# Mixed operands of the first query quad in four steps, key rotation as side work, and VectorE for GpSimd in the operand and rotation work

## The chip, the cores and the metric

The kernel runs on one core of one Trainium2 chip. The metric is the time of one execution on the device in microseconds; the kernel before takes 1295.9 us (median of three runs, 1295.33 to 1296.37).

## The reference

The input `x` is 512 tokens by 1024, float32. One layer is a half-weighted SwiGLU feed-forward block with a layer norm, a token mixer with a layer norm, and a second such feed-forward block.

```python
def swiglu(x, w1, w3, w2):
    return (jax.nn.silu(x @ w1) * (x @ w3)) @ w2
...
    proj = h @ w_in + b_in
    q_a, k_a, v_a, f_h, q_h, i_h, og_h, gate_a, gate_h = jnp.split(proj, splits, axis=-1)
    q_a = partial_rope(q_a.reshape(B, S, N_Q_HEADS, HEAD_DIM), cos, sin)
    k_a = partial_rope(k_a.reshape(B, S, N_KV_HEADS, HEAD_DIM), cos, sin)
    y_attn = sliding_window_attention(q_a, k_a, v_a, sinks)
...
    merged = jax.nn.sigmoid(gate_a) * (y_attn @ w_pa) + jax.nn.sigmoid(gate_h) * (y_hgrn @ w_ph)
    return merged @ w_out
...
    x = layer_norm(DEEPNORM_ALPHA * x + 0.5 * swiglu(x, ffn1_w1[l], ffn1_w3[l], ffn1_w2[l]), ...)
    mix = token_mixer(x, w_in[l], b_in[l], ...)
    x = layer_norm(DEEPNORM_ALPHA * x + mix, ...)
    x = layer_norm(DEEPNORM_ALPHA * x + 0.5 * swiglu(x, ffn2_w1[l], ffn2_w3[l], ffn2_w2[l]), ...)
```

Attention has 16 query heads and 4 key heads of 64, in blocks of 128 tokens with a window of 128 and a learned sink. `y_hgrn` is a gated linear recurrence over eight heads. `partial_rope` rotates the first 16 of each head's 64 entries: with `t` the projection, it is `t * cos + swap(t) * sin`, where `swap` exchanges two groups of eight.

## The kernel before

**Products.** Every float32 operand of a large product is held as a rounded part `hi` and a remainder `lo`; the product is made of three passes, hi by hi, hi by lo and lo by hi. `split` (line 72) makes them: ACT casts to `hi` (line 74), DVE subtracts it from the source to give `lo` (line 75). For weights the names are `whi` and `wlo`, `raw` is the weight as it was loaded (a ring of five), and `wsum` a sum of two of them or a temporary.

**Quads.** The projections of 512 columns by 1024 rows are made with seven products in place of eight (class `Quads`). The activations are cut in four, `b11`, `b12`, `b21`, `b22`, and four mixtures of them are needed too:

```python
t1 = b11 - b12;  t2 = -t1 - b22;  t3 = b22 - b12;  t4 = -t2 - b21
```

`X.mixed` (line 131) forms them on DVE and splits each (`fin`, line 126) into the operands `x1.op["t1"]` to `["t4"]`. The lower part of `t3` and `t4` is formed on GpSimd (POOL), those of `t1` and `t2` on DVE. Its temporaries are rooms of `wsum`, of which there are three, used in turn by `t1`, `t2`, `t4`, `t3` and then by the weight sums. `mixed` is used three times: in the two feed-forward blocks (`ffn`, by way of `Quads.eight`), once each after a block of four products, and in the mixer just before the first query quad.

A quad takes its four raw weights, forms the sums `p1 = w21 + w22` and `p3 = w11 + w21` (`plus`, DVE, line 291), then `p2 = w22 + p3` and `p4 = w12 + p2`, and runs the products in this order, each of 24 matmuls on TensorE (PE, line 278), each with its own activation operand: `f1` (weight w11, operand b11), `f5` (p1, t1), `f6` (p2, t2), `f2` (w12, b21), `f7` (p3, t3), and then in the next quad's `flush` `m4` (w22, t4) and `m3` (p4, b22). After f1 its result is copied by ACT to a room `m` and after f6 to `vs` (`keep`, line 296), since f6 and f7 accumulate into the bank of f1: f6 can't begin before the copy `m` is done, and f7 not before `vs`. `Pipe` prepares one product ahead of the one that runs.

**The mixer's start.** The value projection and `k_half(0)`, `k_half(1)` (the keys, four column blocks in two banks `accs`) run on PE with matmuls of lines 106 to 108. Then stand, in the program, for both key tiles: the bias on ACT (line 646), the rotation (`rope`, lines 645 to 651: a shuffle on DVE, the product with the sines on POOL, the product with the cosines and the sum on DVE), four casts into `k_hi` (ACT, line 685) and two subtractions into `k_lo` (DVE, line 686); then `x1.mixed(quads.sum_room)` and `q_quad(0)`, the first query quad. Rotation of a query tile is the same `rope`; there are ten in all, two for the keys and eight for the queries.

**Order.** A scheduler puts the instructions of each engine in one list, and each engine takes its list in order. `Side` holds generators with small steps of work (rotation of the queries, scores, softmax, outputs) and takes `rate` of them after each product. Attention and the gate quads `gate_quad` (weights `w_ga`, `w_gh`) follow the first query quad so, and the second query quad `q_quad(1)` comes within them. `room(i)` and `big(i)` are buffers named `r` and `g` in the profile.

Of the kernel before, what the change touches and what calls it, by code (L numbers as in the profile page):

```python
# [15 lines left out]
ALU = mybir.AluOpType  # L16
# [26 lines left out]
def body(ctx, tc, a):  # L43
# [73 lines left out]
    class X:  # L117
# [13 lines left out]
        def mixed(self, room):  # L131
            pool = nc.gpsimd
# [3 lines left out]
            def tmp():  # L136
                return room().rearrange("p (k c) -> p k c", k=4)

            t1, t2 = tmp(), tmp()
            nc.vector.tensor_tensor(out=t1, in0=b11, in1=b12, op=ALU.subtract)  # L140
            nc.vector.scalar_tensor_tensor(out=t2, in0=t1, scalar=-1.0, in1=b22, op0=ALU.mult, op1=ALU.subtract)
            self.fin("t1", full, t1)
            t4 = tmp()
            nc.vector.scalar_tensor_tensor(out=t4, in0=t2, scalar=-1.0, in1=b21, op0=ALU.mult, op1=ALU.subtract)
            self.fin("t2", full, t2)
            t3 = tmp()
            nc.vector.tensor_tensor(out=t3, in0=b22, in1=b12, op=ALU.subtract)
            self.fin("t3", full, t3, pool)
            self.fin("t4", full, t4, pool)

# [101 lines left out]
    class Outs:  # L252
# [3 lines left out]
        def room(self, i):  # L256
            return self.rooms[i]
# [4 lines left out]
    class Quads:  # L262
# [60 lines left out]

        def quad(self, src, outs):


            w11, w21, w22, w12 = (raw(src[i]) for i in (0, 2, 3, 1))
            p1 = self.plus(w21, w22)
            p3 = self.plus(w11, w21)
            v, c, m1, vs, u3, p2, p4 = ([] for _ in range(7))  # L330

# [9 lines left out]
            def g2():  # L341
                p2.append(self.plus(w22, p3))
                return wsplit(p2[0])
# [271 lines left out]

    def quad_to(src, d1, d2, done=None):
# [5 lines left out]
        quads.quad(src, Outs((*thalves(d1), d2[:, :, 256:]), finish))  # L622

# [49 lines left out]
    k_hi = [big(i, dtype=F32R) for i in (4, 10)]
    k_lo = [big(i, dtype=F32R) for i in (2, 11)]
    for t in k_lo:
        nc.gpsimd.memset(t[top, 1].bitcast(F32), 0.0)
        nc.gpsimd.memset(t[bot, 0].bitcast(F32), 0.0)
    for j in range(2):  # L680
        t = room(6 + j)
        rope(accs[j], bias("k", j), 1.0, t)
        for h, own in enumerate((top, bot)):
            for half in (top, bot):
                nc.scalar.copy(out=k_hi[j][half, h], in_=t[own])
            nc.vector.tensor_tensor(out=k_lo[j][own, h], in0=t[own], in1=k_hi[j][own, h], op=ALU.subtract)
# [506 lines left out]
```

## Time and profile before

| | us |
|---|---|
| median of three runs | 1295.9 |
| profiled execution | 1297.03 |
| its span, first to last instruction | 1294.9 |
| PE busy | 1253.3 |
| DVE busy | 936.2 |
| ACT busy | 626.4 |
| POOL busy | 75.9 |

The span is the time from the first to the last instruction of the profiled execution, and 2.1 us of the execution lie outside it. The granted clock of TensorE was 0.995 on the mean. In a timeline row an idle time in brackets is what the engine waited before the row, and the name behind the arrow is the instruction whose end it waited for. A row may stand for several instructions of one kind; a matmul's row of eight 128x256 takes 1.12 us at full clock, that is 0.96 us from its first to the next row's start, 0.12 us for each matmul. Twelve matmuls are 1.44 us and a product is 2.88 us.

### The profile page before, as it was taken

The numbers are of one execution on the slowest core, as the hardware profiler recorded it, in microseconds if no ns is written. First come the engines' busy times: TensorE is split into PE (matmuls) and PEld (weight loads), VectorE is DVE, ScalarE is ACT, GpSimd is POOL, SyncE is SP. The second block draws the span as 40 slices with busy tenths as digits, with TensorE's granted clock in tenths as the row PEclk, the third lists the DMA queues.
The fourth block names the chain that finished last, engine by engine and source line by source line (L and its number), as shares of the span: only waits on it lengthen the run. The fifth ranks groups of instructions, "written<-read, shape, count | busy, mean of one in ns | idle before, by whom it ended". The sixth has DMA issues, their size and how long they took to land.

```text
span 1294.9 us, 21771 instructions
## 1 busy us (share of the span) xinstructions
PE 1253.3 (97%) x9040; PEld 1170.0 (90%) x9040; DVE 936.2 (72%) x1288; ACT 626.4 (48%) x891; POOL 75.9 (6%) x53
## 2 busy tenths in 40 slices
PE   7999999999998999999999999899999999999997
PEld 7999999988898989898998987788899999998886
DVE  7987878623499998997778776464798787784325
ACT  5645555411156667667653746342355445463110
POOL 2000000000031100100011010000120000000001
PEclk9999999999999999999999999999999999999998
DMA  6424233532233443223223243574233423354211
GB/s 239 134 96 131 83 114 131 179 96 88 94 104 105 144 134 99 91 98 101 71 77 102 83 130 122 168 255 131 98 115 115 128 85 115 102 162 143 84 47 65
DMA packets 53315, 150.75 MB, mean 116 GB/s; under 512 B 5856, under 2 KB 15072, under 8 KB 53216
## 3 DMA queue, kind: packets, MB, share of 16 engines
q1 hardware_dynamic: 49184, 135.72, 32.3%
q10 hardware_dynamic: 4032, 13.63, 3.0%
q8 instruction: 71, 1.16, 0.4%
q14 instruction: 28, 0.23, 0.1%
HBM read 134.65 MB, written 14.68 MB: 115 GB/s over the span
## 4 chain that ended last, share of the span: by engine, by line
PE 56%; DVE 7%; issue 2%; POOL 1%; ACT 1%; DMA 1%; DVEq 0%; SPq 0%; POOLq 0%; ACTq 0%
PE A L278 30%; PE A L106 4%; PE A L108 4%; PE A L107 4%; PE B L107 2%; PE B L106 2%; PE B L108 2%; PE B L113 2%; PE B L770 1%; DVE wlo L75 1%; PE B L924 1%; POOL rs L968 1%; DVE wsum L291 1%; PE B L926 1%; PE B L728 1%
## 5 line engine op out<-in xcount | busy, mean ns | idle before, releaser
L278 PE MATMUL A<-x,whi 128*128 128x256 f32 x3840 | 550.8, 285 | 14.4 <-ACT whi L74 7.5
L278 PEld LDWEIGHTS A<-x,whi 128*128 128x128 f32 x3840 | 499.9, 193 | 20.1 <-ACT whi L74 7.8
L75 DVE TENSOR_TENSOR wlo<-raw,whi 128x1024 fp32r<-128x1024 f32 (+1 forms) x186 | 225.5, 1214 | 185.3 <-ACT whi L74 184.0
L74 ACT CAST whi<-raw 128x1024 fp32r<-128x1024 f32 (+1 forms) x186 | 192.9, 1040 | 324.2 <-PE A L108 132.0
L278 PE MATMUL A<-x,wlo 128*128 128x256 f32 x1920 | 313.3, 284 | 1.6 <-DVE wlo L75 1.6
L278 PEld LDWEIGHTS A<-x,wlo 128*128 128x128 f32 x1920 | 267.2, 193 | 2.5 <-DVE wlo L75 2.0
L74 ACT CAST whi<-wsum 128x1024 fp32r<-128x1024 f32 x128 | 134.3, 1050 | 153.9 <-PE A L278 96.0
L75 DVE TENSOR_TENSOR wlo<-wsum,whi 128x1024 fp32r<-128x1024 f32 x128 | 156.2, 1220 | 12.5 <-ACT whi L74 12.2
L107 PE MATMUL A<-wlo,x 128*128 128x256 f32 (+1 forms) x360 | 115.4, 321 | 0.0
L106 PE MATMUL A<-whi,x 128*128 128x256 f32 (+1 forms) x360 | 115.3, 320 | 0.0
L108 PE MATMUL A<-whi,x 128*128 128x256 f32 (+1 forms) x360 | 115.0, 320 | 0.0
L291 DVE TENSOR_TENSOR wsum<-raw 128x1024 f32<-128x1024 f32 x64 | 87.6, 1373 | 2.7 <-POOL x L129 2.0
L291 DVE TENSOR_TENSOR wsum<-raw,wsum 128x1024 f32<-128x1024 f32 x64 | 78.0, 1218 | 0.8
L106 PEld LDWEIGHTS A<-whi,x 128*128 128x128 f32 x360 | 68.5, 190 | 5.1
L108 PEld LDWEIGHTS A<-whi,x 128*128 128x128 f32 x360 | 68.3, 190 | 4.9
L107 PEld LDWEIGHTS A<-wlo,x 128*128 128x128 f32 x360 | 68.4, 190 | 4.6
L107 PE MATMUL B<-wlo,x 128*128 128x512 f32 (+1 forms) x200 | 69.8, 349 | 0.0
L106 PE MATMUL B<-whi,x 128*128 128x512 f32 (+1 forms) x200 | 69.6, 348 | 0.0
L108 PE MATMUL B<-whi,x 128*128 128x512 f32 (+1 forms) x200 | 69.3, 347 | 0.0
L412 POOL TENSOR_TENSOR rstd<-ve,pw 128x1 f32<-128x1 f32 x12 | 16.2, 1352 | 759.9 <-DVE ve L410 758.6
L106 PE MATMUL A<-x,whi 128*128 128x512 f32 (+1 forms) x160 | 59.8, 374 | 0.0
L107 PE MATMUL A<-x,whi 128*128 128x512 f32 (+1 forms) x160 | 59.3, 371 | 0.0
(172 smaller groups left out, 1536.6 us busy)
## 6 DMA issues: line engine op xcount, KB each, us to landing
raw<-in_w_dram SPq DMA_DIRECT2D x130, 512.0 KB, 3.6
raw<-in_w_fqg_dram SPq DMA_DIRECT2D x24, 512.0 KB, 3.7
raw<-in_w_q_dram SPq DMA_DIRECT2D x8, 512.0 KB, 3.7
raw<-in_w_ga_dram SPq DMA_DIRECT2D x8, 512.0 KB, 3.4
raw<-in_w_gh_dram SPq DMA_DIRECT2D x8, 512.0 KB, 3.8
raw<-in_w_i_dram SPq DMA_DIRECT2D x8, 512.0 KB, 3.8
raw<-in_w_pa_dram SPq DMA_DIRECT2D x8, 512.0 KB, 4.4
g<-x_spill ACTq DMA_DIRECT2D x8, 512.0 KB, 4.5
```

Of the source, the lines that this page charges most:

```text
L74: nc.scalar.copy(out=hi, in_=src)
L75: nc.vector.tensor_tensor(out=lo, in0=src, in1=hi, op=ALU.subtract)
L106: nc.tensor.matmul(out, lhsT=lh, rhs=rh, start=first, stop=False, **kw)
L107: nc.tensor.matmul(out, lhsT=lh, rhs=rl, start=False, stop=False, **kw)
L108: nc.tensor.matmul(out, lhsT=ll, rhs=rh, start=False, stop=last, **kw)
L113: nc.tensor.transpose(out=tp[:, j * P:(j + 1) * P], in_=b, identity=ident)
L278: nc.tensor.matmul(reg, lhsT=w, rhs=x, start=first, stop=last, skip_group_check=True)
L291: nc.vector.tensor_tensor(out=t, in0=x, in1=y, op=ALU.add)
L412: nc.gpsimd.tensor_tensor(out=rstd, in0=ve, in1=pw, op=ALU.pow)
L728: nc.tensor.matmul(out, lhsT=qs[i][:, hf, qsl], rhs=k_hi[pp][:, hf, ksl], start=True, stop=False)
L770: nc.tensor.matmul(o[hf * HD:(hf + 1) * HD, :256], lhsT=v_sb[:, n + 1 - kb + kk, g * HD:(g + 1) * HD], rhs=pts[kk][:, hf * 256:(hf + 1) * ...
L924: nc.tensor.matmul(sp[:, tsl], lhsT=ei[:, tsl], rhs=q[:, tsl], start=True, stop=True)
```

## The change

`mixed` becomes a generator of four steps, in the order t1, t2, t3, t4, and each step forms its mixture and splits it, all lower parts on DVE. Three rooms are used (t3 takes t1's). In the feed-forward blocks all four steps stand where the call stood before. In the first query quad the steps stand between the weight preparations of the quad: after the preparation of f1, of f5, of f2 and of f7, and `p1` is formed after the first, `p3` after the second. The rooms there are `big(2)`, `big(4)` and `big(10)` in place of the `wsum` rooms.

The keys: the bias goes to `k_raw` straight after `k_half(1)`; rotation and split become the generator `k_parts`, side work with rate 1.0 from the first gate quad on, ahead of attention. The memsets of `k_lo` (POOL) stand in it.

`rope`: the bias is now written by the callers, and the product with the sines is on DVE. Ten products of 128x512 thus go from POOL to DVE, and six lower parts of 128x1024 (two for each of the three uses of `mixed`).

```diff
-        def fin(self, n, c, src, eng=None):
+        def fin(self, n, c, src):
             t = self.op[n][:, :, :, c]
-            nc.scalar.copy(out=t[:, 0], in_=src)
-            (eng or nc.vector).tensor_tensor(out=t[:, 1], in0=src, in1=t[:, 0], op=ALU.subtract)
+            split(t[:, 0], t[:, 1], src)
...
+            t1, t2, t4 = (t.rearrange("p (k c) -> p k c", k=4) for t in rooms)
             nc.vector.tensor_tensor(out=t1, in0=b11, in1=b12, op=ALU.subtract)
+            self.fin("t1", full, t1)
+            yield
...
+            t3 = t1
+            nc.vector.tensor_tensor(out=t3, in0=b22, in1=b12, op=ALU.subtract)
+            self.fin("t3", full, t3)
+            yield
...
-            self.fin("t3", full, t3, pool)
-            self.fin("t4", full, t4, pool)
+            self.fin("t4", full, t4)
+            yield
...
             pipe.push(lambda: wsplit(w11), f1)
+            if mix:
+                next(mix)
+                s1()
             self.flush()
-            pipe.push(lambda: wsplit(p1), f5)
+            pipe.push(lambda: wsplit(p1[0]), f5)
+            if mix:
+                next(mix)
+                s3()
             pipe.push(g2, f6)
             pipe.push(g4, f2)
-            pipe.push(lambda: wsplit(p3), f7)
+            if mix:
+                next(mix)
+            pipe.push(lambda: wsplit(p3[0]), f7)
+            if mix:
+                next(mix)
...
-            self.x.mixed(self.sum_room)
+            for _ in self.x.mixed([self.sum_room() for _ in range(3)]):
+                pass
...
-    def rope(src, b, sign, dst):
-        nc.scalar.activation(out=dst, in_=src, func=AF.Identity, bias=b, scale=sign)
+    def rope(dst):
         rot = room(0)
         nc.vector.stream_shuffle(out=rot, in_=dst, mask=swap)
-        nc.gpsimd.tensor_tensor(out=rot, in0=rot, in1=sin_t, op=ALU.mult)
+        nc.vector.tensor_tensor(out=rot, in0=rot, in1=sin_t, op=ALU.mult)
...
+    k_raw = [room(6 + j) for j in range(2)]
     for j in range(2):
-        t = room(6 + j)
-        rope(accs[j], bias("k", j), 1.0, t)
...
-    x1.mixed(quads.sum_room)
+        nc.scalar.activation(out=k_raw[j], in_=accs[j], func=AF.Identity, bias=bias("k", j), scale=1.0)
+    mix = x1.mixed([big(i, [P, 1024]) for i in (2, 4, 10)])
...
+    def k_parts():
...
+        for j in range(2):
+            t = k_raw[j]
+            rope(t)
+            yield
+            for h, own in enumerate((top, bot)):
+                for half in (top, bot):
+                    nc.scalar.copy(out=k_hi[j][half, h], in_=t[own])
+                nc.vector.tensor_tensor(out=k_lo[j][own, h], in0=t[own], in1=k_hi[j][own, h], op=ALU.subtract)
+                yield
...
-    q_quad(0)
+    q_quad(0, mix)
+    side.add(k_parts())
+    side.rate = 1.0
     gate_quad(0)
```

**DVE at the first query quad, before.** `x_3479` is the operand t2, line 147 forms t3, line 291 is `plus`, `r_3931` the first key tile, `wlo` are weights.

```order
L129 TENSOR_TENSOR x_3479<-wsum,x_3479 128x1024
L147 TENSOR_TENSOR wsum<-g_3475,g_3473 128x1024
L291 TENSOR_TENSOR wsum<-raw 128x1024
L611 TENSOR_TENSOR g_3696<-A,bv_c 128x256
L291 TENSOR_TENSOR wsum<-raw 128x1024
L75 TENSOR_TENSOR wlo<-raw,whi 128x1024
L648 STREAM_SHUFFLE r_3933<-r_3931 128x512
L75 TENSOR_TENSOR wlo<-wsum,whi 128x1024
L650 TENSOR_TENSOR r_3931<-r_3931,rope_c_c 128x512
L291 TENSOR_TENSOR wsum<-raw,wsum 128x1024
L651 TENSOR_TENSOR r_3931<-r_3931,r_3933 128x512
L291 TENSOR_TENSOR wsum<-raw,wsum 128x1024
```

**The same place after.** `x_3478` and `x_3480` are the operands t2 and t3, line 142 forms t3, line 145 t4, line 289 is `plus`.

```order
L142 TENSOR_TENSOR g_3926<-g_3474,g_3472 128x1024
L75 TENSOR_TENSOR wlo<-raw,whi 128x1024
L627 TENSOR_TENSOR g_3695<-A,bv_c 128x256
L75 TENSOR_TENSOR x_3478<-g_3927,x_3478 128x1024
L75 TENSOR_TENSOR wlo<-wsum,whi 128x1024
L289 TENSOR_TENSOR wsum<-raw,wsum 128x1024
L75 TENSOR_TENSOR x_3480<-g_3926,x_3480 128x1024
L289 TENSOR_TENSOR wsum<-raw,wsum 128x1024
L75 TENSOR_TENSOR wlo<-wsum,whi 128x1024
L75 TENSOR_TENSOR wlo<-raw,whi 128x1024
L75 TENSOR_TENSOR wlo<-wsum,whi 128x1024
L145 SCALAR_TENSOR_TENSOR g_3928<-g_3927,g_3473 128x1024
```

The key's shuffle, cosine product and sum (lines 648 to 651 of before) no longer stand between the weights' rows; the lower parts of t2 and t3 and the forming of t4 stand there.

**ACT at the first query quad, before.** `m_4020` is the copy of f1's result.

```order
L74 CAST whi<-wsum 128x1024
L646 ACTIVATE r_3931<-A,b_col_c 128x512
L646 ACTIVATE r_3944<-A,b_col_c 128x512
L74 CAST whi<-wsum 128x1024
L685 CAST g_3923<-r_3931 64x512 x4
L296 COPY m_4020<-A 128x512
L74 CAST whi<-raw 128x1024
L74 CAST whi<-wsum 128x1024
```

**The same place after**, with `m_3977` for that copy; line 690 is the bias of the keys, and `x_3481` is t4's upper part.

```order
L74 CAST whi<-wsum 128x1024
L690 ACTIVATE r_3922<-A,b_col_c 128x512
L74 CAST whi<-wsum 128x1024
L690 ACTIVATE r_3923<-A,b_col_c 128x512
L74 CAST whi<-raw 128x1024
L74 CAST whi<-wsum 128x1024
L294 COPY m_3977<-A 128x512
L74 CAST whi<-raw 128x1024
L74 CAST x_3481<-g_3928 128x1024
```

The four casts of the key tile (line 685) have gone from in front of the copy, and the two weight casts that stood right behind it now stand ahead of it.

**DVE ahead of the first scores, before.** `g_3973` and `g_3974` are the query tiles, line 711 forms a query's lower part, line 733 is the first row of the softmax's maxima (it reads the scores of PE).

```order
L651 TENSOR_TENSOR g_3973<-g_3973,r_4457 128x512
L291 TENSOR_TENSOR wsum<-raw,wsum 128x1024
L711 TENSOR_TENSOR g_4496<-g_3973,g_4496 64x512 x2
L75 TENSOR_TENSOR wlo<-wsum,whi 128x1024
L648 STREAM_SHUFFLE r_4550<-g_3974 128x512
L312 TENSOR_TENSOR r_4490<-vs,A 128x512
L650 TENSOR_TENSOR g_3974<-g_3974,rope_c_c 128x512
L75 TENSOR_TENSOR wlo<-raw,whi 128x1024
L651 TENSOR_TENSOR g_3974<-g_3974,r_4550 128x512
L75 TENSOR_TENSOR wlo<-wsum,whi 128x1024
L733 ISA r_4532,nm<-B,amask_c,nsink 128x128
```

**The same place after**: line 664 is the product with the sines, line 736 the query's lower part, line 758 the maxima.

```order
L736 TENSOR_TENSOR g_4419<-g_3929,g_4419 64x512 x2
L663 STREAM_SHUFFLE r_4455<-g_3929 128x512
L289 TENSOR_TENSOR wsum<-raw,wsum 128x1024
L664 TENSOR_TENSOR r_4455<-r_4455,rope_s_c 128x512
L665 TENSOR_TENSOR g_3929<-g_3929,rope_c_c 128x512
L310 TENSOR_TENSOR r_4488<-vs,A 128x512
L666 TENSOR_TENSOR g_3929<-g_3929,r_4455 128x512
L75 TENSOR_TENSOR wlo<-wsum,whi 128x1024
L736 TENSOR_TENSOR g_4494<-g_3929,g_4494 64x512 x2
L663 STREAM_SHUFFLE r_4548<-g_3930 128x512
L758 ISA r_4530,nm<-B,amask_c,nsink 128x128
```

The sines' products stand in DVE's list, and the third query tile's products with sines and cosines have moved behind the first maxima.

## Rows read from the trace of the kernel before

**Rows 1.** The page, part 1: busy us (share of the span), instructions of each engine.

```profile
PE 1253.3 (97%) x9040; PEld 1170.0 (90%) x9040; DVE 936.2 (72%) x1288; ACT 626.4 (48%) x891; POOL 75.9 (6%) x53
```

**Rows 2.** Waits of PE: who waited, for what: us in total, times, longest.

```profile
PE B L113 <- DVE r L970: 9.4, 7, 2.5
...
PE A L278 <- ACT m L296: 5.8, 3, 3.7
...
PE A L278 <- DVE wlo L75: 1.6, 2, 0.9
```

**Rows 3.** Stretches of 25 us: length, each engine's busy us, granted clock, DMA.

```profile
375.00:400.00 25.00, 20.40 (x158) 19.99 (x158) 22.97 (x23) 13.43 (x16) 11.09 (x4) 0.95 0.15 49
425.00:450.00 25.00, 24.38 (x204) 24.17 (x203) 24.86 (x44) 16.64 (x30) 3.41 (x2) 1.00 0.38 123
500.00:525.00 25.00, 25.00 (x209) 23.70 (x208) 19.50 (x44) 18.17 (x39) 0.00 (x0) 1.00 0.38 114
525.00:550.00 25.00, 23.31 (x173) 21.77 (x172) 24.65 (x51) 16.20 (x36) 5.12 (x3) 0.93 0.28 90
```

**Rows 4.** PE in order of time, first query quad: start, length, [idle before <-releaser].

```profile
386.47 1.12 PE L278 MATMUL A<-x,whi 128*128 128x256 f32 x8
388.54 0.74 PE L278 MATMUL A<-x,wlo 128*128 128x256 f32 x4 [0.95 <-DVE wlo L75]
...
397.24 2.00 PE L278 MATMUL A<-x,whi 128*128 128x256 f32 x8 [3.66 <-ACT m L296]
...
405.62 1.22 PE L278 MATMUL A<-x,whi 128*128 128x256 f32 x8 [0.39 <-ACT vs L296]
```

**Rows 5.** DVE in order of time, first query quad.

```profile
383.94 3.41 DVE L291 TENSOR_TENSOR wsum<-raw 128x1024 f32<-128x1024 f32 x1 [1.96 <-POOL x L129]
...
393.00 0.68 DVE L651 TENSOR_TENSOR r<-r,r 128x512 f32<-128x512 f32 x1
393.61 1.21 DVE L291 TENSOR_TENSOR wsum<-raw,wsum 128x1024 f32<-128x1024 f32 x1
```

**Rows 6.** GpSimd in order of time, first query quad.

```profile
379.45 6.82 POOL L129 TENSOR_TENSOR x<-wsum,x 128x1024 fp32r<-128x1024 f32 x2 [10.34 <-ACT x L128]
389.23 2.16 POOL L649 TENSOR_TENSOR r<-r,rope_s_c 128x512 f32<-128x512 f32 x1 [2.96 <-DVE r L648]
```

**Rows 7.** ACT in order of time, first query quad.

```profile
393.11 1.05 ACT L74 CAST whi<-wsum 128x1024 fp32r<-128x1024 f32 x1 [5.75 <-DVE wsum L291]
394.07 2.51 ACT L685 CAST g<-r 64x512 fp32r<-64x512 f32 x4
396.60 0.59 ACT L296 COPY m<-A 128x512 f32<-128x512 f32 x1
```

**Rows 8.** DVE in order of time, the two FFNs (first at 25.93).

```profile
25.93 6.17 DVE L291 TENSOR_TENSOR wsum<-raw 128x1024 f32<-128x1024 f32 x2
...
954.23 6.20 DVE L291 TENSOR_TENSOR wsum<-raw 128x1024 f32<-128x1024 f32 x2
```

**Rows 9.** PE in order of time, the two FFNs.

```profile
40.05 1.22 PE L278 MATMUL A<-x,whi 128*128 128x256 f32 x8 [1.46 <-ACT m L296]
...
967.40 1.22 PE L278 MATMUL A<-x,whi 128*128 128x256 f32 x8 [0.74 <-ACT m L296]
```

**Rows 10.** One line, L650, the cosines' product of queries: duration ns min/median/max.

```profile
L650 DVE TENSOR_TENSOR g<-g,rope_c_c x8: 676/1346/1772, 423.9 to 560.0; 128x512 f32<-128x512 f32 x8
```

**Rows 11.** DVE in order of time, beside a rotation on GpSimd at 531.78.

```profile
531.66 2.40 DVE L711 TENSOR_TENSOR g<-g,g 64x512 fp32r<-64x512 f32 x2
```

**Rows 12.** PE in order of time, attention.

```profile
448.19 1.22 PE L278 MATMUL A<-x,whi 128*128 128x256 f32 x8 [0.62 <-ACT vs L296]
...
453.27 0.33 PE L113 MATMUL B<-ident,r 128*128 128x128 f32 x1 [2.19 <-DVE r L757]
...
540.06 0.33 PE L728 MATMUL B<-g,g 128*128 128x128 f32 x1 [1.37 <-DVE g L711]
...
541.27 2.02 PE L278 MATMUL A<-x,whi 128*128 128x256 f32 x8
```

More of the change, by code (lines that the diff above doesn't have):

```diff
@@ L124, in __init__, with mixed @@
             self.op = {n: slot(i, [P, 2, 4, 256]) for i, n in enumerate(OPS)}
-        def fin(self, n, c, src, eng=None):
+        def fin(self, n, c, src):
             t = self.op[n][:, :, :, c]
-            nc.scalar.copy(out=t[:, 0], in_=src)
-            (eng or nc.vector).tensor_tensor(out=t[:, 1], in0=src, in1=t[:, 0], op=ALU.subtract)
-        def mixed(self, room):
-            pool = nc.gpsimd
+            split(t[:, 0], t[:, 1], src)
+        def mixed(self, rooms):
             full = slice(0, 256)
             b11, b12, b21, b22 = (self.plain[k] for k in ("b11", "b12", "b21", "b22"))
-            def tmp():
-                return room().rearrange("p (k c) -> p k c", k=4)
-            t1, t2 = tmp(), tmp()
+            t1, t2, t4 = (t.rearrange("p (k c) -> p k c", k=4) for t in rooms)
             nc.vector.tensor_tensor(out=t1, in0=b11, in1=b12, op=ALU.subtract)
+            self.fin("t1", full, t1)
+            yield
             nc.vector.scalar_tensor_tensor(out=t2, in0=t1, scalar=-1.0, in1=b22, op0=ALU.mult, op1=ALU.subtract)
-            self.fin("t1", full, t1)
-            t4 = tmp()
-            nc.vector.scalar_tensor_tensor(out=t4, in0=t2, scalar=-1.0, in1=b21, op0=ALU.mult, op1=ALU.subtract)
-            self.fin("t2", full, t2)
-            t3 = tmp()
-            nc.vector.tensor_tensor(out=t3, in0=b22, in1=b12, op=ALU.subtract)
-            self.fin("t3", full, t3, pool)
-            self.fin("t4", full, t4, pool)
+            self.fin("t2", full, t2)
+            yield
[3 more added lines that the diff above has]
+            yield
+            nc.vector.scalar_tensor_tensor(out=t4, in0=t2, scalar=-1.0, in1=b21, op0=ALU.mult, op1=ALU.subtract)
+            self.fin("t4", full, t4)
+            yield
         def load(self, src):
@@ L322, in done, with quad, s1, s3 @@
             pipe.pump()
-        def quad(self, src, outs):
+        def quad(self, src, outs, mix=None):
             w11, w21, w22, w12 = (raw(src[i]) for i in (0, 2, 3, 1))
-            p1 = self.plus(w21, w22)
-            p3 = self.plus(w11, w21)
-            v, c, m1, vs, u3, p2, p4 = ([] for _ in range(7))
+            v, c, m1, vs, u3, p1, p2, p3, p4 = ([] for _ in range(9))
+            def s1():
+                p1.append(self.plus(w21, w22))
+            def s3():
+                p3.append(self.plus(w11, w21))
             def f1(w):
@@ L341, in g2 @@
             def g2():
-                p2.append(self.plus(w22, p3))
+                p2.append(self.plus(w22, p3[0]))
                 return wsplit(p2[0])
@@ L363, in f7 @@
                 u3.append(self.keep(v[0], "u3"))
+            if not mix:
+                s1()
+                s3()
             pipe.push(lambda: wsplit(w11), f1)
+            if mix:
+                next(mix)
+                s1()
             self.flush()
-            pipe.push(lambda: wsplit(p1), f5)
+            pipe.push(lambda: wsplit(p1[0]), f5)
+            if mix:
+                next(mix)
+                s3()
             pipe.push(g2, f6)
             pipe.push(g4, f2)
-            pipe.push(lambda: wsplit(p3), f7)
+            if mix:
[3 more added lines that the diff above has]
+                next(mix)
             self.late = (v, c, w22, p4, u3, vs, outs)
@@ L614, in body, with quad_to @@
     quads = Quads(x1, mxp)
-    def quad_to(src, d1, d2, done=None):
+    def quad_to(src, d1, d2, done=None, mix=None):
         def finish(v):
@@ L621, in finish @@
                 done()
-        quads.quad(src, Outs((*thalves(d1), d2[:, :, 256:]), finish))
+        quads.quad(src, Outs((*thalves(d1), d2[:, :, 256:]), finish), mix)
     class Pair:
@@ L674, in body, with q_quad @@
     top, bot = slice(0, HD), slice(HD, P)
[L675 to L679, printed above, removed]
-    for j in range(2):
-        t = room(6 + j)
-        rope(accs[j], bias("k", j), 1.0, t)
[L683 to L686, printed above, removed]
-    x1.mixed(quads.sum_room)
+    k_raw = [room(6 + j) for j in range(2)]
+    for j in range(2):
+        nc.scalar.activation(out=k_raw[j], in_=accs[j], func=AF.Identity, bias=bias("k", j), scale=1.0)
+    mix = x1.mixed([big(i, [P, 1024]) for i in (2, 4, 10)])
+    k_hi, k_lo = [], []
+    def k_parts():
+        k_hi.extend(big(i, dtype=F32R) for i in (4, 10))
+        k_lo.extend(big(i, dtype=F32R) for i in (2, 11))
+        for t in k_lo:
+            nc.gpsimd.memset(t[top, 1].bitcast(F32), 0.0)
+            nc.gpsimd.memset(t[bot, 0].bitcast(F32), 0.0)
+        for j in range(2):
[6 more added lines that the diff above has]
+                nc.vector.tensor_tensor(out=k_lo[j][own, h], in0=t[own], in1=k_hi[j][own, h], op=ALU.subtract)
+                yield
     q_raw = {}
-    def q_quad(pp):
+    def q_quad(pp, mix=None):
         d = [big(i) for i in range(2)]
@@ L695, in done @@
             q_raw[pp] = d
-        quad_to(a["w_q"][pp], d[0], d[1], done)
+        quad_to(a["w_q"][pp], d[0], d[1], done, mix)
     def q_parts(pp, ip):
@@ L705, in q_parts @@
             t = q_raw[pp][ip][:, i]
-            rope(t, bias("q", 4 * pp + 2 * ip + i), 1.0 if ip == 0 else -1.0, t)
+            nc.scalar.activation(out=t, in_=t, func=AF.Identity, bias=bias("q", 4 * pp + 2 * ip + i),
+                                 scale=1.0 if ip == 0 else -1.0)
+            rope(t)
             yield
```

## The prediction

> **What bounds the kernel now.** I read the page's first part, then the waits of PE, then windows, then timelines. PE is busy for 1253.3 of 1294.9 us, 97% [rows 1]; only its 41.6 us of idle time, and stretches at a lower clock, can be won. The largest waits are those on L970 (9.4 us, seven) [rows 2], in the recurrent heads, where the change edits nothing; they stay. What the change can touch is in four places.
>
> At the first query quad PE waits three times: 0.95 us for a lower part of a weight, 3.66 us before f6 for the copy of f1's result, 0.39 us for the second copy [rows 4]. The stretch 375 to 400 has only 20.40 us of PE work and a granted clock of 0.95 [rows 3]. The copy itself takes 0.59 us; it was late because ACT stood 5.75 us waiting for a weight sum and then did four key casts of 2.51 us in front of it [rows 7]. The sum was late because of POOL: DVE waited 1.96 us for a `wsum` room that POOL still read, and the next sum took 3.41 us beside POOL's second operation [rows 5, 6]. So the chain is POOL, DVE, ACT, PE.
>
> In both FFNs the same pattern is smaller: two sums of weights take 6.17 and 6.20 us beside POOL's lower parts [rows 8], and PE waits 1.46 and 0.74 us before f6 [rows 9], with 0.65 us for a lower part in the second FFN (the 1.6 us in rows 2 less the 0.95 above).
>
> In attention DVE is nearly full, 24.86 of 25 us from 425 to 450 and 24.65 from 525 to 550, but only 19.50 from 500 to 525 [rows 3]. PE waits there 0.62, 2.19 and 1.37 us (and 0.28 right after the last), and after the last of these eight matmuls took 2.02 us, where f1's first eight take 1.12 [rows 4, 12]: the granted clock fell from 2.4 to 1.2 GHz, and the stretch has 0.93 [rows 3].
>
> **Part by part.**
>
> *POOL's lower parts and the new places of the mixtures, first query quad.* From f1's start (386.47) to f7's (405.62) PE ran 96 matmuls of the four products and 4 of a later one, 19.15 us; at 0.12 us each that is 12.00. So 7.15 us are lost: 5.00 of waits and some 2.15 of slow clock and restarts (at 397.24 eight matmuls took 2.00) [rows 4]. Do all operands come in time? I placed the new lists of DVE and ACT by hand on the old durations (DVE 1.21 per 128x1024, with the next start 1.13 later; ACT 1.05 as in rows 7), from t1 at 372 on. The lower part of w11 ends at 381.6 (f1 needs it from 386.5 on), that of p1 at 384.2 (f5 at 389.4), of p2 at 388.7 (f6 at 392.2), of w12 and p3 at 391.0, and t4's at 395.5. The copy `m`, now behind two weight casts that wait for nothing, ends at 390.2. The smallest margin is 2 us, so I take no wait here and a gain of **7.15 us** at f7. The price if a list slips by more than that is the first of the rivals.
>
> *What DVE gains in the same stretch.* Removed: 1.96 of waiting and 3.41 − 1.21 = 2.20 of stretched work [rows 5]; and what POOL's sine products took from DVE. Eight cosine products have a median of 1.35 us and a least of 0.68 [rows 10]; one whose own time stays short has a longer neighbour: two subtractions took 2.40 us [rows 11], where two of 0.68, started 0.61 apart [rows 5], would take 1.3. I take 0.95 us per rotation, six rotations up to 475: 5.7. Added: two lower parts of 1.21 and six sine products with 0.61 us from start to start (393.00 to 393.61 [rows 5]): 2.42 + 3.66. Net: 9.86 − 6.08 = **3.8 us**. So DVE comes forward by less than PE.
>
> A rule of the Trainium skill weighs on this. By the rows, POOL's product of 389.23 spans 2.16 us [rows 6], and DVE loses about half of that. The Trainium skill, page "SBUF — State Buffer", section "Who interferes with whom", says that a DVE operation with two SBUF inputs and a GpSimd operation that reads SBUF use one port as an exclusive lock, so that the second waits until the first is through; the rows agree with that if half of POOL's span is itself waiting. Against the change speaks "Perfetto Trace Analysis", section "Optimizing Scalar/DVE Operations": where DVE is saturated, work may be handed to GpSimd. The same section adds that between these two it might not help. What the kernel would do if POOL's products were free for DVE is the third rival.
>
> *Key rotation as side work.* The same instructions later: 2 shuffles, 4 products, 2 sums, 4 subtractions on DVE and 8 casts on ACT. They leave the place ahead of f6 (2.51 us of casts there [rows 7]) and go behind the quad, where ACT has 8 of 25 us free (16.64 busy [rows 3]). The cover is that attention's first scores start only some 34 us behind f7. POOL's memsets come in time, nothing else is on POOL.
>
> *Attention up to 475.* PE comes 7.15 us earlier to the first scores; by the same hand placing, the query's lower part that they need is ready only about 1.1 us after PE would want it. At the first transposes (453.27 before, after waits of 0.62 and 2.19 us [rows 12]) PE would be waiting for DVE again, 0.7 to 1.3 us; DVE's new list has the first maxima ahead of one rotation's two products and a lower part that stood ahead before, so that they come forward by more than its 3.8. The transposes' data come at about 446.9, 6.4 us earlier. Bounds: 3.8 (DVE's net) and 7.15 + 0.62 + 2.19 = 9.96 (no wait at all). I take **6.4**, since the placing follows each row; behind 475 DVE has room, and the gain stays.
>
> *The wait at 540.* Idle 1.37 + 0.28; 12 matmuls from 541.27 take 2.66 in place of 1.44, 1.2 more: at most 2.9 us [rows 12]. Three rotations stand just ahead, each with a shorter chain without POOL (0.61 in place of about 2.1) and 0.95 − 0.61 = 0.34 us less DVE time. Between 0 and 2.9 I take **1.5**, half.
>
> *FFNs.* DVE's pair of sums loses 6.17 − 2 × 1.21 = 3.75 of stretching, and two lower parts of 1.21 come on: net 1.3 us earlier in each. That nearly covers the 1.46 us of the first, and in the second the waits of 0.65 and 0.74, since these follow each other and one shift moves both. Nothing else is late next: the second sum feeds the cast ahead of the copy. I take **1.5** and **1.4**; bounds 0 and 1.6 each with restarts.
>
> Sum: 6.4 + 1.5 + 1.5 + 1.4 = 10.8 us. The profiled execution took 1297.0, so 1286.2; it lies 1.1 over the median, so **1285** against 1295.9. With every bound at its best, 9.96 + 2.9 + 1.6 + 1.6 = 16, it is 1280.
>
> **The rivals.**
>
> *First: DVE sets attention's pace, or a part of the copy's wait stays.* Attention gains only DVE's 3.8, and 540 between nothing and 1.5: 3.8 + 0 to 1.5 + 2.9 = 6.7 to 8.2, so 1288 to 1289. For it: DVE at 24.86 of 25. Against: its new order. A stay of half the wait at f6 gives nearly the same, 10.8 − 3.7 + some. Chance 0.20.
>
> *Second: cross waits of the key split (slower).* The key's casts stand on ACT behind copies of PE's results, its subtractions on DVE behind those casts, and weight sums behind the subtractions. Where the copy ahead waits for a product that itself waits for a weight part behind a subtraction, DVE stands up to one product, 2.88 us. There are four subtractions, so up to 11.5 us of a full DVE; behind them wait the sums and lower parts of the gate quad, then PE. If PE stands as long, a stretch at half clock may follow each time, 1.2 us as at 541. Four stands of 2.88 + 1.2 cost 16.3 against 10.8, which makes 1301; it decides from 10.8 / 4 = 2.7 us at each stand, clock included. Against: the first casts come after the copies of f7, whose products need nothing of the keys. Chance 0.06.
>
> *Third: POOL's products were cheap for DVE.* Then DVE in attention would gain 4.16 − 6.08, 1.9 us less than before, attention's 6.4 become −1.9, 540 nothing, and with 2.9 of the FFNs it is 1295: no change. Against: rows 10 and 11. Chance 0.05. The section of the Trainium skill's page "Perfetto Trace Analysis" named above would give this result.
>
> *Fourth: better than the sum.* Attention without waits, 540 wholly recovered: 1280. Chance 0.14.
>
> **How the numbers follow.** The forecast's own case has 0.55 (1282 to 1288), the first rival 0.20, the second 0.06, the third 0.05, the fourth 0.14. A measurement can tell about 0.2%, 2.6 us, from no change. Faster by more than that: 0.55 + 0.20 + 0.14 less a little for an overlap at the edge, 0.87; the same 0.07; slower 0.06. The range of 8 in 10 leaves out the second and third rivals and the far tail of the fourth: 1279 to 1292.
>
> **What would show it.** Right: between f1 and f7 no wait and 12 us; no DVE operation over 1.3 us for 128x1024 in the three places; the copy before f6 in the first FFN no longer waited for. A wait of about 1 us at the first transposes belongs to it. Wrong: a wait at f6 in the quad for a mixture's or sum's part; waits on DVE between 410 and 475 that add up to over 4 us; idle time of DVE ahead of the key's subtractions; a granted clock below 1 in that stretch. The waits on L970 should stay near 9.4 us.

## The result and the profile after

The changed kernel takes 1283.6 us (median of four, 1282.28 to 1284.25) against 1296.1 beside it: 0.990 of the time, 95% interval 0.988 to 0.991, 12.5 us less. 1285 was predicted, with 1279 to 1292 as the range. The profiled execution took 1284.19 us, its span is 1282.3.

The page's first part, as [rows 1]:

```profile
PE 1252.5 (98%) x9040; PEld 1169.5 (91%) x9040; DVE 929.4 (72%) x1304; ACT 625.4 (49%) x891; POOL 38.2 (3%) x37
```

DVE has 16 instructions more and is busy for 6.8 us less: what it no longer loses beside POOL is more than what it took over. The waits of PE, as [rows 2] (who, for what: us in total, times, longest):

```profile
PE A L276 <- ACT whi L74: 8.1, 3, 5.7
PE B L113 <- DVE r L997: 7.6, 7, 1.5
PE B L753 <- DVE g L736: 1.3, 3, 0.8
...
PE B L986 <- DVE r L978: 1.1, 1, 1.1
```

Of the waits for the copy `m` (5.8 us) and for lower parts of weights (1.6) nothing is left; L997 is L970 of before, seven waits there and here (9.4 and 7.6 us). Of the other signs that the prediction named, no DVE operation of 128x1024 takes more than 1.29 us any more, and DVE never stands for more than 0.06 us ahead of a subtraction of the keys. Stretches, as [rows 3] (length, busy us of PE, PE's weight loads, DVE, ACT and POOL, granted clock, DMA share, GB/s):

```profile
375.00:400.00 25.00, 25.00 (x210) 25.00 (x209) 24.79 (x26) 14.42 (x16) 1.04 (x2) 1.00 0.39 126
425.00:450.00 25.00, 23.47 (x189) 22.23 (x188) 24.77 (x54) 17.24 (x36) 0.00 (x0) 1.00 0.31 99
525.00:550.00 25.00, 24.72 (x203) 23.97 (x203) 24.39 (x67) 18.51 (x44) 0.00 (x0) 1.00 0.27 91
750.00:800.00 50.00, 47.58 (x272) 40.27 (x271) 31.40 (x49) 24.72 (x33) 3.79 (x4) 0.93 0.39 128
```

The first query quad runs without a wait, 25.00 of 25 us where it was 20.40. The last line is new: the clock is 0.93 in the recurrent heads, where before it was 1.00. PE in order of time: at the first scores (L753), where the two waits stand that the prediction placed at 1.1 us, at the first transposes (445.37), and in the heads:

```profile
432.42 0.33 PE L753 MATMUL B<-g,g 128*128 128x128 f32 x1 [0.78 <-DVE g L736]
...
433.14 0.33 PE L753 MATMUL B<-g,g 128*128 128x128 f32 x1 [0.28 <-DVE g L736]
...
444.91 0.63 PE L276 MATMUL A<-x,whi 128*128 128x256 f32 x3 [0.42 <-ACT whi L74]
...
445.37 0.27 PE L113 MATMUL B<-ident,r 128*128 128x128 f32 x1
...
788.47 0.66 PE L113 MATMUL B<-ident,r 128*128 128x128 f32 x4 [1.47 <-DVE r L997]
788.96 0.39 PE L951 MATMUL B<-g,g 128*128 128x128 f32 x2
...
791.33 0.80 PE L951 MATMUL B<-g,g 128*128 128x128 f32 x2
```

Two matmuls of L951 take 0.39 us at 788.96 and 0.80 at 791.33; between them the granted clock fell to half, for 6.8 us.

To say where time went I set the timelines of two kernels side by side: the same copies `m` (ACT, one per quad) and the same first product ahead of the second FFN, and how much earlier each comes. The differences between neighbouring places are what each stage won. Parts of the computation are never left out in the kernels below, so that the stages compare. The table is worked out so, all against the profile before; a stage that ends slower has a minus. The first column holds, besides the first FFN's wait, how long PE waits for the first weights, which differs from profile to profile: where the first FFN is the change's, instruction for instruction, the column lies between 0.2 (k12) and 2.4 us (k5). The total belongs to the profiled execution, which lies above the median of its kernel by 4.6 us in k11, 3.5 in k12 and 1.3 in k7, and below it by 2.2 in k6 and 1.2 in k1.

| kernel | start and first FFN | first quad | attention to 516 | about 540 | recurrent heads and after | second FFN | total |
|---|---|---|---|---|---|---|---|
| the change | 1.5 | 6.9 | 0.9 | 2.9 | −1.5 | 1.9 | 12.6 |
| the change, second profile (k12) | 0.2 | 6.9 | 0.9 | 2.9 | −3.4 | 1.9 | 9.4 |
| before + lower parts on DVE (k1) | 1.7 | −0.6 | −2.7 | 1.5 | 0.3 | 1.9 | 2.0 |
| before + sines on DVE (k2) | −0.2 | 1.6 | 2.9 | 2.9 | −0.7 | 0.0 | 6.4 |
| before + both, POOL out (k7) | 3.1 | 0.0 | 2.4 | 2.9 | −3.9 | 1.9 | 6.4 |
| before + keys as side work (k6) | 0.1 | 4.4 | −4.2 | 0.0 | −0.1 | 0.0 | 0.2 |
| the change, sines on POOL (k3) | 2.2 | 6.3 | −3.1 | 0.0 | −0.7 | 1.9 | 6.5 |
| the change, lower parts on POOL (k4) | −0.6 | 5.5 | 0.7 | 2.9 | −1.2 | −0.2 | 7.1 |
| the change, mixtures at once (k5) | 2.4 | 7.2 | 1.0 | 2.9 | −2.1 | 1.9 | 13.3 |
| the change + an idle POOL product (k11) | 1.9 | 6.9 | −5.1 | 0.3 | −3.7 | 1.9 | 2.3 |
| the change, reciprocal root on ACT (k8) | 1.5 | 6.9 | 0.9 | 2.9 | 11.0 | 1.9 | 25.1 |

### The profile page after: what moved, and what is told of

Read it like the earlier page. It is cut to its first block, busy times and chain, and to the rows that moved or that the text cites. A ratio compares the mean times of both kernels' runs of the same rounds, so it can differ in the third digit from the quotient of the medians.

```text
span 1282.3 us, 21730 instructions
## 1 busy us (share of the span) xinstructions
PE 1252.5 (98%) x9040; PEld 1169.5 (91%) x9040; DVE 929.4 (72%) x1304; ACT 625.4 (49%) x891; POOL 38.2 (3%) x37
## 4 chain that ended last, share of the span: by engine, by line
PE 47%; DVE 3%; POOL 1%; ACT 1%; issue 1%; DMA 0%; DVEq 0%; POOLq 0%; ACTq 0%
PE A L276 23%; PE A L106 5%; PE A L107 5%; PE A L108 5%; PE B L107 2%; PE B L106 2%; PE B L108 2%; PE B L113 1%; PE B L951 1%; POOL rs L995 1%; PE B L953 1%; POOL rstd L428 1%; DVE g L433 1%; PE B L984 0%; PE B L986 0%
## 5 line engine op out<-in xcount | busy, mean ns | idle before, releaser
L289 DVE TENSOR_TENSOR wsum<-raw 128x1024 f32<-128x1024 f32 x64 | 77.5, 1219 | 1.5 <-DMA raw<-in_w_fqg_dram 0.9
L108 PE MATMUL A<-x,wlo 128*128 128x512 f32 (+1 forms) x160 | 59.9, 374 | 0.0
```

The lines of the kernel that those rows point to most:

```text
L108: nc.tensor.matmul(out, lhsT=ll, rhs=rh, start=False, stop=last, **kw)
L289: nc.vector.tensor_tensor(out=t, in0=x, in1=y, op=ALU.add)
```

## The experiments

The theory: POOL's operations hold up DVE, DVE is late with a weight sum, ACT with the copy behind it, PE waits; and in attention POOL's products take from a full DVE. The rival: the moves (steps, keys as side work) do the work in the mixer, and POOL's operations cost DVE little.

**k1: lower parts on DVE, alone.**

```diff
-            self.fin("t3", full, t3, pool)
-            self.fin("t4", full, t4, pool)
+            self.fin("t3", full, t3)
+            self.fin("t4", full, t4)
```

> The kernel before with one part of the change: the lower parts of t3 and t4 on DVE in all three places; mixtures still formed at once, keys still ahead of them, sines' products still on POOL. Theory (POOL's lower parts hold up DVE): both FFNs win what the whole change won there, 1.46 and 1.39 us; at the first query quad DVE loses 4.16 us less and gets 2.42 more, so the copy before f6 comes about 1.7 us earlier, behind the key casts still: 2.9 + 1.7 to 2.7, 1290.5 to 1291.5. Rival (the moves do the work, POOL's operations are cheap for DVE): DVE gets 2.4 us more in each place, nothing is won, 1296 to 1298.

Measured: 1295.96 us, 0.999 of before (0.998 to 1.000), 1.5 us less and not 4.6 to 5.6. The FFNs won what was expected. The first quad lost 0.6 us. PE there, k1:

```profile
395.52 2.08 PE L278 MATMUL A<-x,whi 128*128 128x256 f32 x8 [3.48 <-ACT whi L74]
```

The wait before f6 is nearly as long as before, 3.48 for 3.66 [rows 4], but it is now for the cast of p2 (the sum of w22 and p3), no longer for the copy. That sum has become late, since k1 has another list: ahead of it DVE now does seven operations of the keys' rotation and split, where in the kernel before there are two (k7 shows their rows). Attention then lost 2.7 us; no run takes that loss apart.

**k2: the sines' products on DVE, alone.**

```diff
-        nc.gpsimd.tensor_tensor(out=rot, in0=rot, in1=sin_t, op=ALU.mult)
+        nc.vector.tensor_tensor(out=rot, in0=rot, in1=sin_t, op=ALU.mult)
```

> The kernel before with one part of the change: the ten sines' products on DVE, all else as before. Theory: a POOL product costs DVE some 0.95 us and the chain of a rotation about 1.5 us more than a DVE product of 0.61; the wait at 540 goes (2.85 us with its slow clock), the query quad wins 0.5 to 1 us since two rotations stand ahead of the late sum: 1292 to 1293. Rival (POOL's products cheap for DVE, DVE full in attention): ten times 0.61 us more on a full engine, PE waits grow by 1 to 4 us, 1297 to 1300.

Measured: 1290.32 us, 0.995 (0.993 to 0.996), 7.1 us less, twice what was expected. The quad won 1.6 us, 540 the whole 2.9, and attention 2.9 us that the expectation did not have. For the rival of cheap POOL products nothing is left. The copy before f6 is still waited for, 3.14 us, and the transposes wait 0.67 in place of 2.19 [rows 12]:

```profile
396.95 1.22 PE L278 MATMUL A<-x,whi 128*128 128x256 f32 x8 [3.14 <-ACT m L296]
...
449.50 0.52 PE L113 MATMUL B<-ident,r 128*128 128x128 f32 x2 [0.67 <-DVE r L757]
```

**k3: the change with the sines' products back on POOL.**

```diff
-        nc.vector.tensor_tensor(out=rot, in0=rot, in1=sin_t, op=ALU.mult)
+        nc.gpsimd.tensor_tensor(out=rot, in0=rot, in1=sin_t, op=ALU.mult)
```

> The changed kernel with one part undone: the ten sines' products back on POOL. Theory: the wait at 540 with its slow clock comes back, 2.85 us, and a part of what attention gained, 0.5 to 1.5 us: 1287 to 1288. FFNs unchanged. Rival (POOL's products cheap for DVE): DVE is relieved by 0.61 us ten times, 1282 to 1283.6.

Measured: 1290.92 us, 0.995 (0.994 to 0.997), above the 1287 to 1288 expected: 6.5 us less than the kernel before beside it, where the change wins 12.5 to 14. Undoing this one line takes back half of the change's gain. The first quad keeps 6.3 us, attention gives 3.1 of it back, and both waits of before stand there again:

```profile
447.30 0.52 PE L113 MATMUL B<-ident,r 128*128 128x128 f32 x2 [3.24 <-DVE r L782]
...
534.77 0.33 PE L753 MATMUL B<-g,g 128*128 128x128 f32 x1 [1.39 <-DVE g L736]
```

That is the first rival of the prediction, attention at DVE's pace, and it is true of the change without this line.

**k4: the change with the lower parts back on POOL.**

```diff
-            self.fin("t3", full, t3)
+            self.fin("t3", full, t3, nc.gpsimd)
...
-            self.fin("t4", full, t4)
+            self.fin("t4", full, t4, nc.gpsimd)
```

> The changed kernel with one part undone: the lower parts of t3 and t4 back on POOL in all three places, still in steps. Theory: the FFNs' waits come back, 2.85 us together; at the first query quad two POOL operations take some 2 us each from DVE in place of 1.21, which the margin of 2 us ahead of f6 just covers, 0 to 1.5 us: 1286.5 to 1288. Rival (the steps and the moved keys do the work): no more than 0.5 us, 1283.6 to 1284.1.

Measured: 1290.14 us, 0.994 (0.993 to 0.996), 7.3 less than before and some 6 more than the change, where 3 to 4.5 were expected. Both FFN waits are back, the first at 2.07 us even longer than before; in the quad, in steps, the lost part is 1.4 us, behind f7 and not at f6:

```profile
40.68 1.22 PE L277 MATMUL A<-x,whi 128*128 128x256 f32 x8 [2.07 <-ACT m L295]
...
406.51 1.22 PE L277 MATMUL A<-x,whi 128*128 128x256 f32 x8 [1.60 <-ACT u L295]
...
960.33 1.22 PE L277 MATMUL A<-x,whi 128*128 128x256 f32 x8 [0.73 <-ACT m L295]
```

**k5: the change with the mixtures formed at once.**

```diff
-    q_quad(0, mix)
+    for _ in mix:
+        pass
+    q_quad(0)
```

> The changed kernel with one part undone: the four mixtures of the first query quad formed and split all at once ahead of the quad, not between its weights; keys still side work, nothing on POOL. Theory (the key casts and POOL made the copy late, the steps are of little worth): eight DVE operations of 1.13 us from 372 end at about 381, w11's lower part at 383 to 384 (needed at 387.4), p2's some 2 us later than in the changed kernel, at 390.7 (needed at 392.2): no wait or one under 1 us, 1283.6 to 1284.6. Rival (the steps make room for the weights): f1, f5 or f6 wait 2 to 4 us for a lower part and the clock falls once more, 1286 to 1289.

Measured: 1283.45 us, 0.989 (0.988 to 0.991), the same as the change; the quad's stage 7.2 us against 6.9. The first part of the change's title is worth nothing here, and the theory's figure held: even with all eight operations ahead of the weights no weight came late. The stretch of the quad, k5:

```profile
375.00:400.00 25.00, 25.00 (x211) 25.00 (x210) 25.00 (x27) 15.54 (x20) 1.04 (x2) 1.00 0.38 116
```

**k6: the keys as side work, alone.**

```diff
+    def k_parts():
...
+    side.add(k_parts())
+    side.rate = 1.0
     gate_quad(0)
```

> The kernel before with one part of the change: the keys' bias straight behind their products, rotation and split as side work from the first gate quad on. Mixtures at once with lower parts on POOL, sines' products on POOL. Theory: the casts of 2.51 us no longer stand ahead of the copy, and two rotations not ahead of the late sum (some 4 us of DVE), but the sum still waits 4.2 us for POOL: of the quad's 7.15 us some 5 to 6 are won, FFNs nothing, 540 as before: 1290 to 1291.5. Rival (POOL alone makes the copy late): the copy wins 1 to 2 us, 1294 to 1295.

Measured: 1299.05 us (ten runs, 1295.59 to 1302.77), 1.002 of before (1.000 to 1.003). No gain, against 5 expected. The quad did win 4.4 us, with the copy's wait down to 0.68; attention gave back 4.2. PE in order of time, k6:

```profile
394.14 1.22 PE L278 MATMUL A<-x,whi 128*128 128x256 f32 x8 [0.68 <-ACT m L296]
...
447.86 1.50 PE L278 MATMUL A<-x,whi 128*128 128x256 f32 x8 [2.51 <-ACT vs L296]
...
539.75 0.33 PE L737 MATMUL B<-g,g 128*128 128x128 f32 x1 [1.39 <-DVE g L720]
```

The keys' two rotations are only moved into the stretch where DVE is full, and with POOL beside them DVE has no room for them: the same move with POOL out (the change) leaves attention 0.9 us ahead.

**k7: POOL out, nothing moved.** The edits of k1 and k2 together.

> The kernel before with POOL out of the operands and the rotations (lower parts and sines' products on DVE), nothing moved: mixtures at once, keys rotated and split ahead of the quad. Theory: FFNs 2.85, 540 2.85, the quad 2 to 3.5 of its 7.15 since two rotations, four subtractions and four casts still stand ahead of the copy, attention some 1: 1286 to 1288.5. If POOL out were the whole change, 1283.6; if the moves alone were, 1296.

Measured: 1289.07 us, 0.994 (0.992 to 0.995), 7.7 us less; the time is just above what was expected, but the stages are not: the quad won nothing. This is the run that corrects the theory. DVE in order of time before, then DVE, ACT and PE in k7:

```profile
388.42 0.74 DVE L648 STREAM_SHUFFLE r<-r 128x512 f32<-128x512 f32 x1
...
390.16 1.78 DVE L650 TENSOR_TENSOR r<-r,rope_c_c 128x512 f32<-128x512 f32 x1
391.87 1.21 DVE L291 TENSOR_TENSOR wsum<-raw,wsum 128x1024 f32<-128x1024 f32 x1
```

```profile
387.26 0.67 DVE L686 TENSOR_TENSOR g<-r,g 64x512 fp32r<-64x512 f32 x1
...
388.80 0.69 DVE L686 TENSOR_TENSOR g<-r,g 64x512 fp32r<-64x512 f32 x1 [0.20 <-ACT g L685]
389.50 0.69 DVE L649 TENSOR_TENSOR r<-r,rope_s_c 128x512 f32<-128x512 f32 x1
390.11 0.69 DVE L650 TENSOR_TENSOR r<-r,rope_c_c 128x512 f32<-128x512 f32 x1
390.71 1.22 DVE L291 TENSOR_TENSOR wsum<-raw,wsum 128x1024 f32<-128x1024 f32 x1
```

```profile
388.79 0.59 ACT L296 COPY m<-A 128x512 f32<-128x512 f32 x1
391.96 1.05 ACT L74 CAST whi<-wsum 128x1024 fp32r<-128x1024 f32 x1 [2.59 <-DVE wsum L291]
```

```profile
393.06 2.08 PE L278 MATMUL A<-x,whi 128*128 128x256 f32 x8 [3.30 <-ACT whi L74]
```

POOL's lower parts and products are gone. The copy is early (388.79), and PE still waits 3.30 us: for the cast of p2, which waits for the sum at 390.71. In the kernel before, this sum (391.87) stands behind two operations of the keys, the first key's shuffle and its product with the cosines; the list that the scheduler made for k7 has nine ahead of it, the first key's whole rotation and both its subtractions, and of the second key's rotation all but the last sum. So the sum begins only 1.2 us earlier, though k7 comes 3.1 us earlier to the quad. The waits of PE in the quad are 3.8 us against 5.0 of before, but the granted clock falls for longer; the stretch before, then in k7:

```profile
385.00:410.00 25.00, 20.00 (x150) 19.40 (x149) 24.88 (x26) 14.25 (x19) 5.54 (x3) 0.93 0.30 96
```

```profile
385.00:410.00 25.00, 21.18 (x150) 20.49 (x150) 23.14 (x27) 14.76 (x20) 0.00 (x0) 0.86 0.34 118
```

A granted clock of 0.86 over 25 us costs up to 3.5 us, one of 0.93 up to 1.8, so that what the waits won is given back.

With the keys away (k6) 4.4 us come even with POOL in; with POOL out and the keys there (k7) none; with both 7.2 (k5) or 6.9 (the change). So without the keys' move POOL out is worth nothing in the quad, and with it 2.5 to 2.8 us. k5 and k7 differ in the rooms of the mixtures too, but ahead of the late sum DVE in k7 waits for no room (0.29 us for a key's bias, 0.20 for a key's cast).

**k11: an idle POOL product beside each rotation.**

```diff
         nc.vector.tensor_tensor(out=dst, in0=dst, in1=rot, op=ALU.add)
+        nc.gpsimd.tensor_tensor(out=room(5), in0=dst, in1=sin_t, op=ALU.mult)
```

> The changed kernel, and after each of the ten rotations one more product of 128x512 on POOL, of two operands in SBUF, whose result nothing reads; DVE's list is the same as in the changed kernel. It separates what a POOL product takes from DVE by running beside it from what it cost as a link of the rotation's chain. If DVE is held up by about 1 us each (POOL beside it), six of ten lie in the full stretch 400 to 475 and attention gives back 2 to 5 us, and some of the wait at 540 returns: 1285.5 to 1289. If it was the longer chain alone, nothing changes: 1283 to 1284.

Measured: 1289.89 us, 0.995 (0.994 to 0.997), 6.1 us more than the change beside it and just above what was expected for a delayed DVE. Nothing on DVE waits for the result and DVE's list is the same, yet this loses nearly as much as the sines on POOL (k3, 7.3 us above the change). The two subtractions of a query, in the change and then in k11, and POOL and PE in k11:

```profile
424.81 1.40 DVE L736 TENSOR_TENSOR g<-g,g 64x512 fp32r<-64x512 f32 x2
```

```profile
425.69 2.38 DVE L737 TENSOR_TENSOR g<-g,g 64x512 fp32r<-64x512 f32 x2
...
433.53 2.35 DVE L737 TENSOR_TENSOR g<-g,g 64x512 fp32r<-64x512 f32 x2
```

```profile
424.67 2.14 POOL L667 TENSOR_TENSOR r<-g,rope_s_c 128x512 f32<-128x512 f32 x1 [14.24 <-DVE g L666]
```

```profile
435.21 0.48 PE L754 MATMUL B<-g,g 128*128 128x128 f32 x1 [3.79 <-DVE g L737]
```

DVE loses 0.98 and 0.95 us in these two, and over all ten products it is busy 7.2 us longer than in the change (936.6 against 929.4), 0.7 on the mean. PE's wait at the first scores, 0.78 in the change, is 3.79, and the granted clock is 0.86 from 425 to 450, where the change has 1.00. This is a price of running beside POOL, not of a longer chain. The profiled execution is the slowest of five, so the stages of the table lose more than the 6.1 us of the medians. One use of `room(5)` by attention's outputs is shared with the idle product, which may hold something of the later part; the rows above lie ahead of the first output.

**k8: the reciprocal root on ACT, beyond the change.**

```diff
-        nc.gpsimd.tensor_tensor(out=rs, in0=ss, in1=pw.broadcast_to([P, TT]), op=ALU.pow)
+        func(out=rs, in_=ss, func=AF.Ln)
+        func(out=rs, in_=rs, func=AF.Exp, scale=-0.5)
```

> The changed kernel, and beyond it the reciprocal root of the recurrent heads' norm as a logarithm and an exponential on ACT in place of POOL's power (eight times, L995). It measures what is left there: PE waits 7.6 us in seven places behind it, and in the changed kernel's profile the clock halves for 6.8 us right behind the wait of 1.47 at 788. If POOL's 1.39 us is what PE waits for, two small ACT operations of some 0.25 us win 0.8 us or more in each of seven places and the slow stretch goes, 1277 to 1280. If ACT's list is the longer way (casts of 1.05 us stand in it), no gain or a loss, 1283 to 1287.

Measured: 1271.46 us, 0.980 (0.978 to 0.982), 25 us less than before and 12 less than the change; better than the best that was expected. The waits behind it are gone from the list, and the stretch that had clock 0.93 has 1.00. Waits of PE, ACT in order of time, and the stretch, k8:

```profile
PE A L276 <- ACT whi L74: 7.6, 3, 5.7
PE B L753 <- DVE g L736: 1.3, 3, 0.8
PE B L113 <- DVE g L433: 1.2, 4, 0.4
```

```profile
686.15 0.20 ACT L193 ACTIVATE rs<-ss 128x4 f32<-128x4 f32 x1 [1.16 <-DVE ss L993]
686.39 0.20 ACT L193 ACTIVATE rs<-rs 128x4 f32<-128x4 f32 x1
```

```profile
750.00:800.00 50.00, 49.69 (x289) 41.45 (x288) 35.13 (x54) 27.40 (x40) 2.35 (x2) 1.00 0.38 125
```

Two operations of 0.20 us stand in place of one of POOL, which has 1.39 us on the mean in the change:

```profile
L995 POOL TENSOR_TENSOR rs<-ss,pw 128x4 f32<-128x4 f32 x8 | 11.1, 1387 | 81.7 <-DVE ss L993 81.7
```

The heads win 11.0 us against before and 12.5 against the change. The change's waits there, 7.6 on L997 and 1.1 on L986, are 8.7 of that; 6.8 us at half clock cost some 3.4 more, and 0.4 is left for restarts. In the kernel before, whose heads ran at full clock, the waits of these two kinds (9.4 and 1.1) are 10.5 of the 11.0.

**k9: k8 with the mixtures at once.**

> The kernel with the reciprocal root on ACT (k8) and the four mixtures formed at once (k5). If the steps are worth nothing, 1270.5 to 1272; if they were worth something that k5's heads or start hid, 1272.5 or more. It is the candidate for the best version.

Measured: 1271.92 us, 0.981 (0.979 to 0.982): the same as k8. The steps are worth nothing with the heads undisturbed too. k8 and k9 are the best versions, and no run tells them apart.

**k12: the change again.**

> The changed kernel once more, with a second profile. Where the clock halves for 6.8 us behind a wait of the recurrent heads in the first profile (at 790), does it again, and is all ahead of it the same? Expected: 1282.5 to 1284.5, the same gains up to 620 within 0.3 us; the slow stretch in the heads at the same wait, at another, or absent.

Measured: 1283.77 us, 0.989 (0.988 to 0.991). From the first quad to 540 the second profile has the same gains to 0.1 us. The start came 1.3 us later and the heads lost 1.9 us more, with the clock at half for 10.2 us from 807 in place of 6.8 from 790. The stretch, k12:

```profile
800.00:820.00 20.00, 17.47 (x79) 13.96 (x77) 7.16 (x12) 4.73 (x8) 1.01 (x1) 0.74 0.23 73
```

## Why the prediction was right, and where its steps were not

*The first quad*: 7.15 us were predicted, 6.9 measured. The size was right, the reason only in part, and that the number fits is partly luck. The chain "POOL, DVE, ACT, PE" is in the rows of the kernel before. But the prediction put the gain down to POOL's lower parts and the new places of the mixtures, and named, of the keys' work ahead of f6, only ACT's casts. k7 takes POOL away and wins nothing, k6 takes the keys' work away and wins 4.4, k5 forms the mixtures at once and loses nothing. What the reading overlooked is the keys' work in DVE's list: with it there, the sum p2 is late without POOL too. The new lists placed by hand had this work away already, so the number came out right.

*The steps*: the prediction took the hand placing of the new lists as it was and never asked what the lists would be without the steps. k5 and k9 show no difference.

*The sines*: DVE's gain per rotation was taken as 0.95 us of loss. k11 has 0.98 and 0.95 beside two subtractions but 0.7 on the mean of ten: the mechanism is right, the size somewhat high.

*Attention*: 6.4 us were predicted to be left at 475; the quad and attention to 516 give 6.9 + 0.9 = 7.9. The wait at the first scores was placed at 1.1 us and is 0.78 + 0.28 = 1.06. The term that was mis-sized is the wait at the first transposes, 0.7 to 1.3 us; there is none, their data are in time. PE waits just ahead of them instead, 0.42 us at 444.91 for the cast of a weight.

*540*: half of the 2.9 us was taken; all of it came (2.9 in the change, and in k2 by the sines alone). The wait for the query's lower part is 0.28 us in place of 1.37, and the granted clock of 525 to 550 is 1.00 in place of 0.93.

*FFNs*: 1.5 and 1.4 predicted, 1.5 and 1.9 measured, the second with the restarts of its two waits. The first figure holds the start of the kernel too, which alone moves it between 0.2 and 2.4, so that its agreement is luck; what is shown is that the wait of 1.46 us before f6 is gone. k1 and k4 show that POOL's lower parts are their whole cause, here as predicted.

*What was not foreseen*: the heads. The waits on L970 were put down as untouched, near 9.4 us; there are seven still, of 7.6 us in the first profile and 9.1 in the second. But what follows them is not the same. In the change's first profile 1.5 us went there, in its second 3.4, behind stretches at half clock that the profile before did not have in this place. Two of the change's first four executions have a mean clock of 0.998 and take 1282.28 and 1283.0, the other two 0.996 and 1284.19 and 1284.25. Why the clock falls behind one of these waits in some executions and not in others stays open; k8, where the waits are gone, has no such stretch.

*The sum*: 10.8 us predicted for the profiled span, 12.6 measured: 1.5 more up to 516, the quad included, 1.4 more at 540, 0.5 more in the second FFN, and 1.5 lost in the heads; that is 12.7, the 12.6 but for rounding. That the total came so near is in part luck, since the loss in the heads hides nearly half of what the terms had too low.

*The rivals*: attention at DVE's pace (0.20) did not come about in the change, but it is what k3, k6 and k11 show: with POOL's products in attention DVE gives back 3 to 5 us. Cross waits of the key split (0.06): none; DVE waits at most 0.06 us ahead of the four subtractions. Cheap POOL products (0.05): fell with k2, k3 and k11. The rule behind that rival, in the Trainium skill's "Perfetto Trace Analysis", section "Optimizing Scalar/DVE Operations", that a saturated DVE's work may go to GpSimd, is not borne out for two-input products: DVE at 24.8 of 25 us took them back and the kernel became 6 to 7 us faster; the section's own reserve about these two engines is what the runs show. The Trainium skill's "SBUF — State Buffer", section "Who interferes with whom", with its exclusive lock, agrees: in k11 POOL's span is 2.14 us where its shortest is 1.27, and DVE's loss beside it is 0.98, as if each of the two stood for a part while the other worked.

## What to carry to other kernels

A list of waits names the last link that was late, and of several works in an engine's list any may be the one that counts: take them away one at a time, since here POOL out alone and the keys moved alone won 0.0 and 4.4 us in the quad and both together 6.9 to 7.2. And look at the list that each kernel got: in k7 the place that POOL's work had left was taken by other work ahead of the same sum. A move that wins at one place only lasts if the engine that has to take the work up has room; k6 won 4.4 us and had lost them 50 us later. And a small operation (1.39 us on POOL, eight times, on a chain that PE waits for) can cost as much as sixteen large ones: k8 wins 12 us more, about what the whole change did.

## What was not expected of the hardware

Ten POOL products of 128x512 whose results nothing reads cost DVE 7.2 us (up to 1.0 each) and the kernel 6 us, nearly as much as ten that stand in the chain. Short waits in the heads are dearer than their length: waits of 8.7 us in all gave 12.5 when they went, since the clock falls behind some of them, 6.8 us at half in one profile and 10.2 in another of the same kernel, and in another place; the profile before has such waits too (9.4 us) and no fall there.
